# A recurrence's gates one weight chunk later, a compressor's tanh ahead of the second half of q and k, in a two-layer hybrid decoder

## Chip, cores and metric

One core of a Trainium2 chip. The time is device microseconds of one execution of the whole program; before the change the median of three runs is 248.72. The engines are named as the profile names them: PE (matrix products), DVE (vector engine), ACT (scalar engine), POOL and SP.

## The reference, cut to what matters

Two layers. Each makes one input projection and feeds two mixers from it: a gated recurrence of width 512 (RG-LRU) and an attention of 8 query heads and 2 key/value heads with three branches (compressed blocks, selected blocks, sliding window). Both are gated, joined and projected back onto the residual. SEQ is 256, D_MODEL 1024, everything float32.

```python
def rg_lru(x, w_r, b_r, w_i, b_i, lam):
    B, S, C = x.shape
    xb = x.reshape(B, S, RG_BLOCKS, RG_BLOCK)
    r = jax.nn.sigmoid(jnp.einsum('bsnc,ncd->bsnd', xb, w_r).reshape(B, S, C) + b_r)
    i = jax.nn.sigmoid(jnp.einsum('bsnc,ncd->bsnd', xb, w_i).reshape(B, S, C) + b_i)
    log_a = (-RG_C * r.astype(jnp.float32)) * jax.nn.softplus(-lam.astype(jnp.float32))
    a = jnp.exp(log_a)
    u = jnp.sqrt(-jnp.expm1(2.0 * log_a)) * (i * x).astype(jnp.float32)
    ...
    _, h = lax.associative_scan(combine, (a, u), axis=1)
    return h.astype(x.dtype)

def compress_blocks(blocks, pe, w1, w2):
    z = (blocks + pe).reshape(blocks.shape[:-2] + (CMP_LEN * HEAD_DIM,))
    return jax.nn.silu(z @ w1) @ w2

def hybrid_layer(x, norm_g, w_in, ...):
    h = rms_norm(x, norm_g)
    z = h @ w_in
    ...
    y_a = rg_lru(causal_depthwise_conv(rg_x, conv_w, conv_b), rg_wr, rg_br, rg_wi, rg_bi, rg_lam)
    y_a = y_a * jax.nn.silu(rg_gate)
    y_b = nsa(q, k_c, v_c, k_s, v_s, k_w, v_w, br_gate, q_g, k_g, ...)
    y_b = y_b * jax.nn.silu(nsa_gate)
    y = jnp.concatenate([y_a, y_b], axis=-1)
    return x + y @ w_out
```

With 256 positions there are 4 blocks of 64, and up to 16 may be chosen, so every block is selected, so the selected and the window branch attend to all earlier positions; the kernel computes both side by side.

## The kernel before

All of the weights stream through the core. A weight chunk is loaded by DMA, cut into a rounded high part and a low remainder (L170, a DVE operation of 128 x 1024 for most chunks), and multiplied in three passes (L175 to L177), which is what a `mm3` is: high by high, high by low, low by high.

A layer is a list of steps, one weight chunk each. First eight chunks `wt` give q and the keys token by token, then `wc` and `wv` the compressor's inputs and the values, then twelve chunks `wf` of 24 matmuls each, which give the recurrence's input (x0 to x3), the attention's gate (n0 to n3) and the recurrence's gate (g0 to g3), and at last eight chunks `wo` of the output projection. `SL` is the plan of the layer's small work: for each piece the number of the chunk, counted from the first `wf` chunk, in front of which it is given out (with `mid` after the loads, still ahead of the products). The lines 782 to 807 turn `SL` into lists, in the order in which `at` is called; two pieces with the same number stand in that order. The Tile layer then sorts the instructions of each engine by its own list scheduler, so the order in the program is not that of the source word for word, and each engine runs its list strictly in order.

The pieces that the change and the prediction's steps touch:

- `qk_transpose(t)`, for one half of the tokens: PE turns the keys (L371) and queries (L380); ACT rounds the keys twice (L375, L376) and the queries (L384, twice); DVE writes the low halves, `kl` (L377) and the lower 64 rows of `qs` (L385, twice); ACT copies the queries once more (`qT`, L387). In layer 0 the second half is given out in front of chunk 2, in layer 1 in front of chunk 1 (`SL["qk"][1] - l`).
- the compressor: `cmp_act` multiplies the hidden vectors by a selection matrix (L468, PE), takes a tanh (`hth`, L470, ACT) and the product `hs` (L472, DVE). `cmp_kv` multiplies `hs` by the second weights (L477, L478, PE) and normalises the compressed keys (L482 to L495); `cmp_kt` turns them (L499, L501). `cmp_scores` (L511 to L533) and `cmp_pt` (L538, and a copy `pct`, L83) follow. In `SL` these three are `cmp=(2, 3, 4)`.
- `att_scores`: scores of a head pair (L581 to L583 on PE, reading `kd`, `kl` and all of `qs`), the negated maximum (L586, L588, DVE), the exponential (L594, ACT). `att_coef`: L599 and L600 on DVE, then the scaling L609 on ACT. `att_turn`: transposes L622 and copies L83. `att_out`: L636 to L642 and L644.
- the recurrence: `rg_x(j)` frees the projection's PSUM bank (L654, DVE) and convolves (L655 ACT, three L657 DVE). `rg_gates(j)`: two products L665 on PE, four functions on ACT (L668, L669, L671, L672), and for odd j L675 and L678 on DVE and a square, L677, on ACT. `rg_sqrt`: one square root of 128 x 1024 on ACT (L681), for which a table is loaded (ACT_TABLE_LOAD) and another one loaded back before the next exponential. Then the scan (L686) and the gated output (L690).

PSUM banks: the chunk products and the gate products share the two banks `fm` in turn; `m` is one bank, `pp` two, `s` three.

Of the kernel before, what the change touches and what calls it, by code (L numbers as in the profile page):

```python
# [38 lines left out]
for _n, _w in (("g", 8), ("cw", 16), ("cb", 4), ("br", 4), ("bi", 4), ("lam", 4)):  # L39
# [12 lines left out]
K = dict(scale="A", ev1="A", hid="A", pct="A")  # L52
SL = dict(qk=(0, 2), order=("x0", "x1", "x2", "x3", "n0", "n1", "g0", "g1", "g2", "g3", "n2", "n3"),
          cmp=(2, 3, 4), att=(1, 3, 3, 4, 6, 7, 10, 11), turn=(3, 4, 5, 6, 8, 10,
          12, 13), cs=(5, 5), cpt=6, aout=(7, 15), gates=(2, 3, 4, 5), tab=6, sqrt=5,
          scan=8, rout=(9, 11))


# [13 lines left out]
def hybrid_trunk_kernel(ctx: ExitStack, tc: tile.TileContext, vx, wc, wt, wv, wf, wo, w1, w2, pe,  # L72
# [185 lines left out]
    def layer(l, prev):  # L258
# [520 lines left out]
        def at(n, f, *a, mid=False):  # L779
            plan[n][1 if mid else 0].append(F(f, *a))  # L780

        at(1, cmp_hid)
        at(SL["qk"][0], qk_transpose, 0)
        at(SL["qk"][1] - l, qk_transpose, 1)
        for n, f in zip(SL["cmp"], (cmp_act, cmp_kv, cmp_kt)):
            at(n, f)
        for q in range(8):
            i, t = divmod(q, 2)
            n = SL["att"][q]
# [34 lines left out]
    for l in range(DEPTH):  # L824
        prev, st_ = layer(l, prev)
        prev0 = prev0 or prev
        steps += st_
# [140 lines left out]
```

## Time and profile before

| | us |
|---|---|
| median of three runs | 248.72 (248.48 to 249.34) |
| the profiled execution, its own time | 248.43 |
| its span in the trace | 246.6 |
| PE busy in the span | 240.6 |
| DVE busy | 195.6 |
| ACT busy | 163.8 |

The span is what the trace covers from the first to the last instruction; 1.83 us of the profiled execution lie around it. Busy times overlap, since the engines work side by side. A share of PE near one says that a matmul was in its pipe nearly always, also while the next one was held back a little. The clock that PE was granted is at its full level in all forty slices of the page.

### The profile page before, as it was taken

What the parts mean: (1) busy time and instruction counts of PE and PEld (TensorE: products, weight loads), DVE (VectorE), ACT (ScalarE), POOL (GpSimd) and SP (SyncE); (2) the same over time, 40 slices, a digit from 0 to 9 for tenths busy, and PEclk for the clock granted to TensorE, in tenths of its full rate; (3) what the DMA queues carried; (4) which work ended last, traced back from release to release, by engine and by line L of the source; (5) the groups of instructions that cost most, each with busy time, mean ns of one, the idle gap of its engine ahead of it and who ended that gap; (6) DMA issues with size and microseconds to landing.
All of it is one profiled execution on the core that took longest, in us unless ns stands there. A gap on an engine that the chain in (4) does not pass through costs nothing.

```text
span 246.6 us, 5201 instructions
## 1 busy us (share of the span) xinstructions
PE 240.6 (98%) x1958; PEld 222.2 (90%) x1958; DVE 195.6 (79%) x379; ACT 163.8 (66%) x414; POOL 38.8 (16%) x65
## 2 busy tenths in 40 slices
PE   8999999989999999999999999999999999999994
PEld 3989998978998899979999999987899979998993
DVE  5997897999999988555995569699997999865322
ACT  6965529799999878523863453778999998760100
POOL 0035450012600011000001044101100101110000
PEclk9999999999999999999999999999999999999999
DMA  6988999774789388851479878558559675870022
GB/s 219 358 296 267 347 412 406 258 237 144 248 321 403 116 287 309 244 167 48 144 227 350 306 237 255 182 170 241 193 187 346 229 258 159 292 229 6 3 85 85
DMA packets 17593, 57.17 MB, mean 232 GB/s; under 512 B 2208, under 2 KB 3360, under 8 KB 17056
## 3 DMA queue, kind: packets, MB, share of 16 engines
q1 hardware_dynamic: 12816, 39.86, 46.8%
q0 software_dynamic: 4608, 16.78, 21.5%
q8 instruction: 15, 0.25, 0.4%
q10 hardware_dynamic: 144, 0.20, 0.2%
q14 instruction: 10, 0.08, 0.1%
HBM read 55.78 MB, written 1.05 MB: 230 GB/s over the span
## 4 chain that ended last, share of the span: by engine, by line
PE 81%; DVE 10%; ACT 4%; issue 2%; DMA 1%; DVEq 0%; ACTq 0%
PE fm L175 14%; PE fm L177 13%; PE fm L176 13%; PE pp L622 4%; PE s L176 4%; PE s L177 4%; PE s L175 4%; PE m L636 3%; DVE wl L170 2%; PE s L582 2%; PE s L581 2%; PE fm L665 2%; DVE qs L385 2%; PE pp L177 2%; PE pp L176 2%
## 5 line engine op out<-in xcount | busy, mean ns | idle before, releaser
L170 DVE TENSOR_TENSOR wl<-raw,wh 128x1024 fp32r<-128x1024 f32 (+4 forms) x67 | 74.3, 1114 | 7.8 <-PE pp L176 2.9
L175 PE MATMUL fm<-hh,wh 128*128 128x256 f32 x192 | 56.9, 296 | 0.1
L177 PE MATMUL fm<-hh,wl 128*128 128x256 f32 x192 | 54.7, 285 | 0.0
L176 PE MATMUL fm<-hl,wh 128*128 128x256 f32 x192 | 54.6, 285 | 0.0
L167 ACT CAST wh<-raw 128x768 fp32r<-128x768 f32 (+4 forms) x34 | 30.4, 898 | 26.3 <-DMA raw<-in_wc_dram 6.8
L175 PEld LDWEIGHTS fm<-hh,wh 128*128 128x128 f32 x192 | 36.7, 191 | 1.9 <-issue 1.2
L176 PEld LDWEIGHTS fm<-hl,wh 128*128 128x128 f32 x192 | 36.7, 191 | 0.2
L177 PEld LDWEIGHTS fm<-hh,wl 128*128 128x128 f32 x192 | 36.7, 191 | 0.2 <-DVE wl L170 0.2
L594 ACT ACTIVATE pr<-s,sm 128x128 f32<-128x128 f32 (+1 forms) x64 | 26.2, 424 | 2.7 <-DVE sm L588 1.9
L175 PE MATMUL fm<-yy,wh 128*128 128x256 f32 x96 | 27.4, 285 | 0.0
L176 PE MATMUL fm<-yy,wh 128*128 128x256 f32 x96 | 26.8, 279 | 0.0
L177 PE MATMUL fm<-yy,wl 128*128 128x256 f32 x96 | 26.8, 279 | 0.0
L609 ACT ACTIVATE pr<-pr,sm 128x128 f32<-128x128 f32 (+1 forms) x64 | 23.9, 458 | 2.3 <-DVE sm L600 2.3
L175 PEld LDWEIGHTS fm<-yy,wh 128*128 128x128 f32 x96 | 18.0, 188 | 0.8 <-issue 0.8
L156 POOL DMA_DIRECT2D wh<-in_wo_dram x16 | 8.4, 527 | 62.7 <-PE fm L177 28.0
L176 PEld LDWEIGHTS fm<-yy,wh 128*128 128x128 f32 x96 | 18.1, 188 | 0.0
L177 PEld LDWEIGHTS fm<-yy,wl 128*128 128x128 f32 x96 | 18.0, 188 | 0.0
L156 POOL DMA_DIRECT2D wh<-in_wf_dram x16 | 9.0, 563 | 49.7 <-PE fm L177 17.0
L176 PE MATMUL s<-wl,hh 128*128 128x384 f32 x48 | 16.5, 344 | 0.3 <-DVE wl L170 0.3
L177 PE MATMUL s<-wh,hl 128*128 128x384 f32 x48 | 16.2, 337 | 0.0
L175 PE MATMUL s<-wh,hh 128*128 128x384 f32 x48 | 15.5, 346 | 0.0
L731 DVE TENSOR_TENSOR head<-head,fm 128x512 f32<-128x512 f32 x11 | 7.5, 686 | 9.7 <-PE fm L177 9.6
(206 smaller groups left out, 612.6 us busy)
## 6 DMA issues: line engine op xcount, KB each, us to landing
raw<-in_wf_dram SPq DMA_DIRECT2D x24, 512.0 KB, 4.9
wh<-in_wf_dram POOLq DMA_DIRECT2D x16, 512.0 KB, 4.9
raw<-in_wo_dram SPq DMA_DIRECT2D x16, 512.0 KB, 5.3
wh<-in_wo_dram POOLq DMA_DIRECT2D x16, 512.0 KB, 5.0
raw<-in_wt_dram SPq DMA_DIRECT2D x15, 384.0 KB, 4.1
yy<-in_w_dram SPq DMA_DIRECT2D x4, 1024.0 KB, 7.0
raw<-in_wc_dram SPq DMA_DIRECT2D x4, 512.0 KB, 4.8
raw<-in_wv_dram SPq DMA_DIRECT2D x4, 420.0 KB, 4.6
```

The lines of the kernel that those rows point to most:

```text
L156: G.dma_start(self.wh, self.src)
L167: A.copy(hi[:, c], self.raw[:, c])
L170: V.tensor_tensor(lo[:, c], self.raw[:, c], hi[:, c].bitcast(F32), op=ALU.subtract)
L175: T.matmul(o, lh, rh, start=start, stop=False)
L176: T.matmul(o, lh, rl, start=False, stop=False)
L177: T.matmul(o, ll, rh, start=False, stop=stop)
L385: L.qk_done[t] = V.tensor_tensor(L.qs[HD:, g::2, tok], src, L.qs[:HD, g::2, tok].bitcast(F32), op=ALU.subtract)
L594: A.activation(pr[g][:, b], ov[:, b], AF.Exp, bias=sm[:, 0, 2 * g + b:2 * g + b + 1], accum_out=sm[:, 1, 2 * g + b:2 * g + b + 1])
L609: A.activation(pr[g][:, b], pr[g][:, b], AF.Copy, scale=sc_)
L622: T.transpose(pp[:, (2 * g + b) * P:(2 * g + b + 1) * P], pr[g][:, b, c * P:(c + 1) * P], ident)
L636: T.matmul(o[g * HD:(g + 1) * HD], L.vv[:, 0, b, g * HD:(g + 1) * HD], pt[:, g, b, 0:2].rearrange("p a s -> p (a s)"), start=h == b == 0, ...
L731: V.tensor_tensor(x_sb[:, m], x_sb[:, m], os_[0].rearrange("p (a s) -> p a s", a=2), op=ALU.add)
```

## The change

The `wf` chunks 2 to 5 (counted from 0) had one gate step each ahead of them (`gates=(2, 3, 4, 5)`); these four steps go one chunk further on, and the square root with them, from 5 to 6. Apart from that, `cmp_act` keeps its number but is given out before the second half of `qk_transpose` instead of behind it. In layer 1 the second half of q and k is already one chunk ahead of `cmp_act`, so there the second part of the diff changes nothing.

```diff
--- before.py
+++ after.py
@@ -52,7 +52,7 @@
 SL = dict(qk=(0, 2), order=("x0", "x1", "x2", "x3", "n0", "n1", "g0", "g1", "g2", "g3", "n2", "n3"),
           cmp=(2, 3, 4), att=(1, 3, 3, 4, 6, 7, 10, 11), turn=(3, 4, 5, 6, 8, 10,
-          12, 13), cs=(5, 5), cpt=6, aout=(7, 15), gates=(2, 3, 4, 5), tab=6, sqrt=5,
+          12, 13), cs=(5, 5), cpt=6, aout=(7, 15), gates=(3, 4, 5, 6), tab=6, sqrt=6,
           scan=8, rout=(9, 11))
@@ -781,8 +781,9 @@
         at(1, cmp_hid)
         at(SL["qk"][0], qk_transpose, 0)
+        at(SL["cmp"][0], cmp_act)
         at(SL["qk"][1] - l, qk_transpose, 1)
-        for n, f in zip(SL["cmp"], (cmp_act, cmp_kv, cmp_kt)):
+        for n, f in zip(SL["cmp"][1:], (cmp_kv, cmp_kt)):
             at(n, f)
```

What becomes of it in the engines' lists is seen at three places. On PE in layer 0, in front of the third `wf` chunk (+ is the changed kernel, - the kernel before; the line numbers up to L783 are the same in both):

```order
 L177 MATMUL fm<-hh,wl 128x256
+L468 MATMUL m<-cst,hid 128x160
 L371 MATMUL pp<-cst,pt 128x128 x2
 L380 MATMUL pp<-cst,pt 128x128 x4
-L468 MATMUL m<-cst,hid 128x160
-L665 MATMUL fm<-cx,rws 128x256 x2
```

The hidden vectors' product goes ahead of the six transposes, and the first gate's two products leave this place.

On DVE in layer 0, at the same time:

```order
 L654 TENSOR_TENSOR xpad_72<-fm,rb 128x256
 L600 TENSOR_TENSOR sm<-gate,sm 128x4
+L472 SCALAR_TENSOR_TENSOR hs<-hth,m 128x160
+L657 SCALAR_TENSOR_TENSOR cx<-xpad_72,head,cx 128x256
 L377 TENSOR_TENSOR kl<-pp,kd_122 64x2x128
 L657 SCALAR_TENSOR_TENSOR cx<-xpad_72,head,cx 128x256
```

`hs` is now ahead of the low halves of the keys and queries (L377, L385); before, it stood behind both L385.

On ACT in layer 0 around the square root, before the change:

```order
L594 ACTIVATE pr,sm<-s,sm 128x128
L681 ACT_TABLE_LOAD
L681 ACTIVATE tl<-tl 128x1024
L83 COPY pct<-m 128x256
L83 COPY pt<-pp 128x4x128 x2
L609 ACTIVATE pr<-pr,sm 128x128 x4
L594 ACT_TABLE_LOAD
L594 ACTIVATE pr,sm<-s,sm 128x256 x4
```

and after it:

```order
L83 COPY pt<-pp 128x4x128 x2
L668 ACTIVATE rr<-fm,hb 128x256
L669 ACTIVATE tmp_998<-fm,hb 128x256
L83 COPY pct<-m 128x256
L671 ACTIVATE tl<-rr,sp 128x256
L594 ACTIVATE pr,sm<-s,sm 128x256
L672 ACTIVATE rr<-rr,sp 128x256
L609 ACTIVATE pr<-pr,sm 128x128
L677 ACTIVATE tmp_1076<-rr 128x512
L609 ACTIVATE pr<-pr,sm 128x128 x3
L681 ACT_TABLE_LOAD
L681 ACTIVATE tl<-tl 128x1024
```

The table load and the square root stand behind the copies `pct` and `pt`, the fourth gate's functions and the scaling of a head pair, instead of in front of them.

## Rows read from the trace of the kernel before

**Rows 1.** The page: busy us of each engine, share of span, instructions.

```profile
PE 240.6 (98%) x1958; PEld 222.2 (90%) x1958; DVE 195.6 (79%) x379; ACT 163.8 (66%) x414; POOL 38.8 (16%) x65
```

**Rows 2.** Waits of PE: engine line, waited for: us in total, times, longest.

```profile
PE m L113 <- DVE wz L110: 1.1, 1, 1.1
PE m L477 <- DVE hs L472: 0.8, 1, 0.8
```

**Rows 3.** Timeline of PE, layer 0: start us, us, engine, line, what.

```profile
47.44 1.03 PE L665 MATMUL fm<-cx,rws 128*128 128x256 f32 x4
48.12 0.47 PE L175 MATMUL fm<-hh,wh 128*128 128x256 f32 x1
48.42 0.28 PE L176 MATMUL fm<-hl,wh 128*128 128x256 f32 x1
...
51.06 0.28 PE L177 MATMUL fm<-hh,wl 128*128 128x256 f32 x1
51.18 0.40 PE L581 MATMUL s<-kd,qs 128*128 128x512 f32 x1
52.42 0.30 PE L477 MATMUL m<-w2s,hs 128*32 128x64 f32 x2 [0.85 <-DVE hs L472]
...
53.26 0.48 PE L581 MATMUL s<-kd,qs 128*128 128x512 f32 x1
```

**Rows 4.** Timeline of ACT, same stretch.

```profile
49.95 0.30 ACT L470 ACTIVATE hth<-m 128x160 f32<-128x160 f32 x1
50.15 0.47 ACT L668 ACTIVATE rr<-fm,hb 128x256 f32<-128x256 f32 x1
50.64 0.58 ACT L384 CAST qs<-pp 64x512 fp32r<-64x512 f32 x1
```

**Rows 5.** Timeline of DVE, same stretch.

```profile
51.32 0.69 DVE L385 TENSOR_TENSOR qs<-pp,qs 64x512 fp32r<-64x512 f32 x1
52.05 0.32 DVE L472 SCALAR_TENSOR_TENSOR hs<-hth,m 128x160 f32<-128x160 f32 x1
```

**Rows 6.** Busy us by stretch: PE, PEld, DVE, ACT, POOL, PEclk, DMA share, GB/s.

```profile
60.00:70.00 10.00, 10.00 (x82) 9.04 (x81) 9.90 (x18) 10.00 (x32) 5.19 (x11) 1.00 0.75 241
...
100.00:110.00 10.00, 10.00 (x95) 9.21 (x96) 6.16 (x7) 3.28 (x6) 0.53 (x1) 1.00 0.68 202
```

**Rows 7.** Timeline of PE, the same place in layer 1.

```profile
165.98 1.03 PE L665 MATMUL fm<-cx,rws 128*128 128x256 f32 x4
167.09 0.39 PE L175 MATMUL fm<-hh,wh 128*128 128x256 f32 x1
...
170.16 0.30 PE L477 MATMUL m<-w2s,hs 128*32 128x64 f32 x2
...
170.63 0.48 PE L581 MATMUL s<-kd,qs 128*128 128x512 f32 x1
...
171.23 0.48 PE L581 MATMUL s<-kd,qs 128*128 128x512 f32 x1
```

**Rows 8.** Timeline of PE, layer 0: first output products, next pair's transposes.

```profile
78.60 0.65 PE L636 MATMUL m<-pt,vv 128*64 128x256 f32 x4
...
89.58 1.04 PE L622 MATMUL pp<-cst,pr 128*128 128x128 f32 x8
```

**Rows 9.** Timeline of DVE, layer 1.

```profile
166.61 0.42 DVE L654 TENSOR_TENSOR xpad<-fm,rb 128x256 f32<-128x256 f32 x1
...
169.75 0.31 DVE L472 SCALAR_TENSOR_TENSOR hs<-hth,m 128x160 f32<-128x160 f32 x1
```

**Rows 10.** Timeline of ACT, layer 0, round the square root.

```profile
75.47 0.20 ACT L594 ACTIVATION_READ_ACCUMULATOR pr<-s,sm 128x1 f32 x1
75.70 1.28 ACT L681 ACT_TABLE_LOAD   x1
76.99 1.06 ACT L681 ACTIVATE tl<-tl 128x1024 f32<-128x1024 f32 x1
77.96 0.35 ACT L83 COPY pct<-m 128x256 f32<-128x256 f32 x1
```

**Rows 11.** Timeline of ACT, layer 1, gate functions.

```profile
185.32 0.52 ACT L668 ACTIVATE rr<-fm,hb 128x256 f32<-128x256 f32 x1
...
186.53 0.55 ACT L609 ACTIVATE pr<-pr,sm 128x256 f32<-128x256 f32 x1
```

**Rows 12.** Timeline of ACT, layer 0, scaling of the next head pair.

```profile
86.47 1.71 ACT L609 ACTIVATE pr<-pr,sm 128x256 f32<-128x256 f32 x4 [1.26 <-DVE sm L600]
```

## The prediction, made before the changed kernel was run

> **What bounds the kernel now.** I read the busy shares first, then what the Tensor engine (PE) waited for, and then the timelines round those waits. The page gives PE 240.6 of the 246.6 us span [rows 1]. That share counts a matmul that is in the pipe, so it says only that PE is the engine to watch; what PE lost is found in its waits. Beside the warm-up at the start, one wait of PE on another engine is near a microsecond: L477, the compressor's second product, waits 0.8 us for `hs` of the Vector engine (DVE) [rows 2]. It lies in layer 0: the scores' first matmul starts at 51.18, L477 at 52.42, where matmuls otherwise follow each other by 0.12 [rows 3]. Nobody else delayed that much; so what the change can win lies here and in small delays.
>
> Why was `hs` late? On the Scalar engine (ACT) the tanh L470 ran at 49.95, behind the copies of the second half of q and k, and the recurrence's first tanh L668 (0.49 from start to start) then stood in front of the second L384 at 50.64 [rows 4]. DVE, which works its list in order, took L385 (waiting for that L384) at 51.32 and only then L472 (`hs`) at 52.05 [rows 5]. Both helpers are full: from 60 to 70 us DVE is busy 9.90 of 10 and ACT 10.00; from 100 to 110 they are at 6.16 and 3.28 [rows 6]. Work that PE doesn't need soon can therefore be put off, up to a point.
>
> **The change, part by part: layer 0.** Two things are taken from in front of `hs`: its matmul L468 now precedes the transposes L371 and L380, with the tanh ahead of the casts on ACT and `hs` ahead of both L385; and the first gate's product (0.68 us on PE, 47.44 to 48.12 [rows 3]) with its four functions goes one chunk later. `hs` then needs L470 and a 0.32 us DVE operation early in the chunk, some 2 us before PE wants it. That stall is gone. What is late next is the second half of the queries. PE can start the chunk at 47.44 and needs 3.06 for it (48.12 to 51.18 [rows 3]), so 50.50. The two compressor products take 0.47 and the first score group 0.60 (170.16 to 170.63 to 171.23, the same work in layer 1 [rows 7]); two transposes take about 0.2 (a quarter of what eight take, 1.04 with the end of the pipe [rows 8]). PE thus stands at the second score group at 51.77, and that reads what the second L385 writes. L385 ended at 52.01 before [rows 5]. In the new order `hs` (0.32) is ahead of it, which could make it 52.3; on ACT the tanh still precedes, but L668's 0.49 is gone, which could make it 51.7. I take 52.1, since DVE is the fuller chain: a new wait of about 0.3, between 0 and 0.55. Before, the same group began at 53.26 [rows 3], with the gate's 0.68 already done and the two transposes not: 53.26 - 0.68 + 0.2 = 52.78. Gain 52.78 - 52.1 = 0.7, between 0.5 and 1.0.
>
> Something is given back. The new order cuts PE's work into more pieces: the second gate's two products are parted by L499 and a score group, the first head's transposes stand in two pairs, the eight transposes of the next head in four pairs between scores, and L538 falls inside a run of weight matmuls; I count six new breaks. A return to weight matmuls costs at most 0.18 (48.12 to 48.42 is 0.30, against 0.12 from 51.06 to 51.18 [rows 3]), and may cost nothing where the other product is as long as its load: 0 to 1.1 in all. Most of these breaks lie between transposes and scores, not before weight matmuls, so I take 0.05 each, 0.3. Layer 0: 0.7 - 0.3 = 0.4 faster.
>
> **Layer 1.** There L468 already stood early, and only the gates move. Before, the first gate's product and the wait behind it took 1.11 (165.98 to 167.09 [rows 7]), 0.43 more than 0.68: the third x chunk's bank was being read by L654, which ended at 167.03 [rows 9]. In the new order that chunk uses the other bank and starts at 165.98. With 3.07 (167.09 to 170.16) and one score group of 0.60 that now stands ahead, PE is at L477 at 169.65. But `hs` ends at 170.06, held by DVE's own list [rows 9], which doesn't change up to there. So PE waits 0.41: the removed wait comes back under another name. By 170.1 PE has done 0.60 of scores in place of 0.68 of gate: no gain, no loss. Later the order has up to two breaks fewer; I take 0.05 faster, at most 0.36.
>
> **What costs nothing, and what hides it.** The fourth gate's functions and the square root now come after the first copies of the output stage. The copy of `pct` on ACT ended at 78.31 and PE read it at 78.60 [rows 8, 10]: 0.29 of cover. PE now comes there eleven matmuls, 1.3 us, sooner, but ACT no longer has the table load and square root (75.70 to 77.96, 2.26 us [rows 10]) ahead of that copy, and has two of the gate's functions instead (0.8 by [rows 11]: two of three that take 1.21). Net cover about 0.3 + 2.26 - 0.8 - 1.3 = 0.45; without it PE would pay what is missing. The scan's results are wanted only by the output projection, far behind. No DMA is moved to another queue, and the Pool engine's order is the same.
>
> The sum: 0.4 + 0.05 = 0.45 faster. Against the profiled execution's own 248.43 that is 247.98; its span is 246.6, with 1.83 around it that I leave as it is. That execution is 0.29 below the median of the runs, 248.72, to which I apply the same difference: 248.27, rounded to **248.3**. About 0.3%, 0.75 us, is what a measurement of this kernel can tell from no change, so the forecast is "the same".
>
> **The rivals.** *Nothing is given back.* The qs half comes by 51.77, the breaks are free and layer 1 saves its 0.36: 1.0 + 0.36 = 1.36 faster, 247.4; for this speaks that the order has work at hand at each break, against it the DVE at 9.9 of 10 [rows 6].
>
> *The square root pushes the next head pair's exponentials (slower).* The switch pair now stands behind the fourth gate. Three gate functions took 1.21 (185.32 to 186.53 [rows 11]); four and the pair's square, at 0.4 each, are 2.0. The exponentials behind the second table load, then the scaling L609 and at last the transposes L622 would come up to 2.0 later. L609 ended at 88.18 (86.47 + 1.71 [rows 12]) and PE began those transposes at 89.58 [rows 8]: 1.40 of cover. Beyond that PE waits, up to 0.6 in each layer, and if the 0.45 cover of `pct` goes with it since it hangs on the same ACT list, another 0.4: 1.6 in all, 1.6 - 0.45 = 1.15 slower, 249.9. For it speaks ACT's full list [rows 6]; against it that ACT had 1.26 us of idle just before that L609 [rows 12], which would take up most of it. It decides from a slip of 1.4 us.
>
> *The chip pays more for a switch at its new place.* A table load took 1.28 at 75.70, and the ACT instruction before it ended at 75.67 [rows 10], so nothing but the load is seen. Were each of the four switches to cost its 1.28 once more, past the cover, the time would be 248.3 + 5.1 = 253.4. The Trainium skill, ScalarE: Activation LUTs (What ACT_TABLE_LOAD costs), says that a switch pays a drain of about 1.38 us beside the load of 1.28; by that an estimate for four switches would be 5.5 us more. The trace agrees with its load, and shows no such drain.
>
> *It doesn't do what it says.* `hs` comes early, but L385 comes so much later that PE stands as long as before: 248.7.
>
> **How the numbers follow.** Forecast 0.55 (own range 247.8 to 249.3: a gain of 1.0 with breaks of 0.2 at the one end, of 0.5 with breaks of 1.1 at the other). Nothing given back 0.27; square root 0.12; switch 0.02; no effect 0.04. The range goes from 247.4, the first rival, to 249.6, short of the full price of the second, which leaves about 2 in 10 out. Faster by over 0.3%: 0.27 and 0.03 of the forecast's lower edge, 0.30. Slower: 0.12 + 0.02 + 0.03 of its upper edge, 0.17. Within: 0.53.
>
> **What would show it.** Right: no wait of L477 on `hs` in layer 0, and a short one of a score matmul L581 on L385 there; in layer 1 a wait of about 0.4 of L477 on `hs` and none of L175 on L654. Wrong: a PE wait on L609 behind the square root, or on the copy of `pct`; or, if faster, no wait at L581. If the time is over 249.6 with none of these, my count of breaks is wrong.

## The result, and the profile of the changed kernel

The changed kernel takes 250.55 us (median of five runs, 250.04 to 251.27) against 248.63 for the kernel before in the same measurement: a ratio of 1.0066, interval 1.0046 to 1.0087. It is slower by 1.9 us in the medians and 1.6 by the ratio, where 248.3 was forecast and the range ended at 249.6. Its profiled execution took 250.04, with a span of 248.2.

The page still shows PE as the engine that is nearly always busy (busy us of each engine, share, instructions), which says as little as it did before [rows 1]:

```profile
PE 242.1 (98%) x1958; PEld 222.5 (90%) x1958; DVE 194.4 (78%) x379; ACT 164.1 (66%) x414; POOL 39.4 (16%) x65
```

The waits of PE (us in total, times, longest) look harmless too; `L477` still waits for `hs`, though not where it did [rows 2]:

```profile
PE m L113 <- DVE wz L110: 1.1, 1, 1.1
PE m L477 <- DVE hs L472: 0.5, 1, 0.5
PE s L176 <- DVE wl L170: 0.2, 1, 0.2
PE s L581 <- DVE qs L385: 0.2, 1, 0.2
```

Beside the wait at the start, which was there before, no wait of a microsecond stands in this list, so the list is not enough. What finds it is to follow the same matmul through both traces. The weight matmuls stand in the same order in all programs here, so the first one of a chunk marks a stage. The first row gives the time of each mark in the trace of before, the other rows how much longer each stage took than there (us; "after again" is a second trace of the changed kernel, e1 to e10 are the experiments below).

| kernel | start to first `wf` | layer 0, to first `wo` | to third `wo` | to layer 1's first `wf` | layer 1, to first `wo` | to third `wo` | median of runs |
|---|---|---|---|---|---|---|---|
| before (time of the mark) | 37.05 | 97.75 | 104.31 | 155.52 | 215.67 | 222.23 | 248.6 |
| after | +0.23 | -0.29 | **+1.01** | 0.00 | +0.29 | +0.36 | 250.55 |
| after again | +1.03 | -0.25 | **+1.04** | +0.03 | +0.30 | +0.36 | 250.22 |
| e1 tanh only | +0.02 | +0.41 | 0.00 | 0.00 | -0.01 | 0.00 | 248.82 |
| e2 gates only | +0.59 | +0.48 | +1.11 | 0.00 | +0.29 | +0.35 | 250.65 |
| e3 gate 4, sqrt back | +0.09 | +1.35 | 0.00 | 0.00 | +1.33 | +0.37 | 251.53 |
| e4 sqrt only | +0.29 | +0.01 | +0.37 | 0.00 | +0.14 | 0.00 | 249.17 |
| e5 coefficients first | +0.16 | -0.28 | +0.23 | 0.00 | +0.30 | +0.47 | 249.40 |
| e7 layer 0 only | -0.10 | -0.02 | +0.23 | 0.00 | +0.01 | 0.00 | 248.56 |
| e8 short scan | -0.10 | -0.23 | +0.37 | 0.00 | +0.29 | 0.00 | 249.02 |
| e9 hs early in layer 1 | -0.06 | -0.29 | +0.23 | +0.10 | -0.01 | +0.32 | 248.82 |
| e10 the same, other end | +0.14 | -0.28 | +0.23 | 0.00 | -0.02 | +0.49 | 249.19 |

What follows the third `wo` chunk of layer 1 is within 0.02 of before in every trace. The first stage lies ahead of every instruction that the change moves, and its scatter (0.23 and 1.03 in two traces of one and the same program) is chance. The same goes for the first `wf` chunk of layer 0, the beginning of the second stage: in all these programs the order on every engine is that of before up to 46 us. The rest of the changed kernel adds up to -0.29 + 1.01 + 0.29 + 0.36 = 1.37, in its second trace to 1.48. So the gain in layer 0 is there, and more than it is lost in three places: at the end of that layer (1.01), in the middle of layer 1 (0.29) and at its end (0.36).

**The stretch that costs most.** PE in front of the second `wo` chunk of layer 0, before (timeline: start us, us, engine, line, what):

```profile
97.75 0.36 PE L175 MATMUL fm<-yy,wh 128*128 128x256 f32 x1
...
100.63 1.03 PE L622 MATMUL pp<-cst,pr 128*128 128x128 f32 x8
101.42 0.37 PE L175 MATMUL fm<-yy,wh 128*128 128x256 f32 x1
```

and after:

```profile
97.69 0.36 PE L175 MATMUL fm<-yy,wh 128*128 128x256 f32 x1
...
100.88 1.74 PE L622 MATMUL pp<-cst,pr 128*128 128x128 f32 x8
102.37 0.36 PE L175 MATMUL fm<-yy,wh 128*128 128x256 f32 x1
```

From 97.69 to 102.37 are 4.68 us, against 3.67 before. The eight transposes come 0.3 later behind the first matmul shown (3.19 in place of 2.88) and take 1.49 to the next matmul in place of 0.79. They read what the scaling L609 writes. On ACT, before:

```profile
97.11 0.21 ACT L594 ACTIVATION_READ_ACCUMULATOR pr<-s,sm 128x1 f32 x1
97.83 1.71 ACT L609 ACTIVATE pr<-pr,sm 128x256 f32<-128x256 f32 x4 [0.50 <-DVE sm L600]
```

and after:

```profile
98.25 0.47 ACT L594 ACTIVATE pr<-s,sm 128x256 f32<-128x256 f32 x1
98.61 0.20 ACT L594 ACTIVATION_READ_ACCUMULATOR pr<-s,sm 128x1 f32 x1
98.70 0.58 ACT L83 COPY pt<-pp 128x512 f32<-128x512 f32 x1
99.17 0.65 ACT L546 ACTIVATE sgn<-tmp 128x512 f32<-128x512 f32 x1
100.31 1.71 ACT L609 ACTIVATE pr<-pr,sm 128x256 f32<-128x256 f32 x4 [0.50 <-DVE sm L600]
```

Before, this L609 started at 97.83, so 2.8 us ahead of PE's first transpose; now it starts 0.57 ahead, and PE is paced by its four parts of some 0.4 us each. L609 waits for the coefficients L600 of the last head pair. DVE, after:

```profile
96.95 1.22 DVE L170 TENSOR_TENSOR wl<-raw,wh 128x1024 fp32r<-128x1024 f32 x1
98.09 0.68 DVE L544 TENSOR_TENSOR tmp<-fm,rb 128x512 f32<-128x512 f32 x1
98.84 0.18 DVE L599 RECIPROCAL sm<-sm 128x4 f32<-128x4 f32 x1
98.93 1.21 DVE L170 TENSOR_TENSOR wl<-raw,wh 128x1024 fp32r<-128x1024 f32 x1
100.06 0.16 DVE L600 TENSOR_TENSOR sm<-gate,sm 128x4 f32<-128x4 f32 x1
```

and before:

```profile
97.36 0.18 DVE L599 RECIPROCAL sm<-sm 128x4 f32<-128x4 f32 x1 [0.80 <-ACT pr L594]
97.57 0.16 DVE L600 TENSOR_TENSOR sm<-gate,sm 128x4 f32<-128x4 f32 x1
```

L600 is 2.5 us later. Some 1.5 of that go with the exponentials L594, whose sums L599 needs and which end 1.5 later (98.81 against 97.32). The other 1.0 come from one weight split, L170, that now stands between L599 and L600 in DVE's list (1.22 from L599 to L600 in place of 0.21), and which PE does not need yet.

What went ahead of that? The busy windows (us; PE, PEld, DVE, ACT, POOL busy, each with its instructions, then PE's clock, DMA share, GB/s), before:

```profile
77.00:83.00 6.00, 6.00 (x60) 4.76 (x60) 5.78 (x12) 5.97 (x14) 0.00 (x0) 1.00 0.63 237
83.00:100.00 17.00, 17.00 (x142) 16.36 (x141) 14.58 (x25) 13.32 (x42) 2.64 (x5) 1.00 0.79 263
```

After:

```profile
77.00:83.00 6.00, 6.00 (x62) 4.76 (x60) 2.61 (x6) 5.95 (x13) 0.05 (x1) 1.00 0.53 184
83.00:100.00 17.00, 17.00 (x142) 16.36 (x141) 16.93 (x28) 13.70 (x41) 2.59 (x5) 1.00 0.73 231
```

From 77 to 83 us DVE, which worked 5.78 us before, works 2.61: it waits for the fourth gate's square on ACT, for the output products, and for the square root (waits of DVE there):

```profile
DVE tl L678 <- ACT tmp L677: 1.5, 1, 1.5
DVE cx L682 <- ACT tl L681: 0.9, 1, 0.9
DVE tmp L644 <- PE m L642: 0.9, 1, 0.9
```

The product with the root (L682, at 82.60 in place of 78.46) and the four scans behind it then fall into the next 17 us, where DVE has 16.93 us of work and no gap left to catch up in. The change took work from a full stretch of DVE, left a hole, and put the work into a stretch that had just 2.4 us to spare. The trace shows this backlog; it doesn't show whether the backlog made the coefficients late, or the order that the scheduler gave to the work.

### The profile page after: what moved, and what is told of

Same layout as the page of the kernel before. It is cut to its first block, busy times and chain, and to the rows that moved or that the text cites. A ratio compares the mean times of both kernels' runs of the same rounds, so it can differ in the third digit from the quotient of the medians.

```text
span 248.2 us, 5193 instructions
## 1 busy us (share of the span) xinstructions
PE 242.1 (98%) x1958; PEld 222.5 (90%) x1958; DVE 194.4 (78%) x379; ACT 164.1 (66%) x414; POOL 39.4 (16%) x65
## 4 chain that ended last, share of the span: by engine, by line
PE 65%; DVE 16%; ACT 13%; issue 2%; DMA 2%; SPq 0%; DVEq 0%; ACTq 0%
PE fm L175 10%; PE fm L176 10%; PE fm L177 10%; DVE wl L170 5%; PE s L176 4%; PE s L177 4%; PE s L175 4%; PE pp L622 3%; PE fm L665 2%; PE m L636 2%; ACT pr L609 2%; ACT pr L594 2%; DVE qs L385 2%; DMA raw<-in_wt_dram 2%; PE s L581 2%
## 5 line engine op out<-in xcount | busy, mean ns | idle before, releaser
L170 DVE TENSOR_TENSOR wl<-raw,wh 128x1024 fp32r<-128x1024 f32 (+4 forms) x67 | 74.2, 1112 | 7.0 <-PE pp L176 3.8
L175 PE MATMUL fm<-hh,wh 128*128 128x256 f32 x192 | 57.0, 297 | 0.0
L175 PEld LDWEIGHTS fm<-hh,wh 128*128 128x128 f32 x192 | 36.7, 191 | 1.4 <-issue 1.2
L594 ACT ACTIVATE pr<-s,sm 128x128 f32<-128x128 f32 (+1 forms) x64 | 26.1, 423 | 2.2 <-DVE sm L588 1.9
L175 PE MATMUL fm<-yy,wh 128*128 128x256 f32 x96 | 27.3, 285 | 0.0
L609 ACT ACTIVATE pr<-pr,sm 128x128 f32<-128x128 f32 (+1 forms) x64 | 24.2, 460 | 3.0 <-DVE sm L600 3.0
L175 PEld LDWEIGHTS fm<-yy,wh 128*128 128x128 f32 x96 | 18.1, 188 | 0.8 <-issue 0.8
L562 ACT CAST yy<-tmp 128x512 fp32r<-128x512 f32 x8 | 5.0, 622 | 17.8 <-DVE tmp L644 12.7
```

The source lines that it names most:

```text
L170: V.tensor_tensor(lo[:, c], self.raw[:, c], hi[:, c].bitcast(F32), op=ALU.subtract)
L175: T.matmul(o, lh, rh, start=start, stop=False)
L562: A.copy(L.yy[:, 0, k], yt)
L594: A.activation(pr[g][:, b], ov[:, b], AF.Exp, bias=sm[:, 0, 2 * g + b:2 * g + b + 1], accum_out=sm[:, 1, 2 * g + b:2 * g + b + 1])
L609: A.activation(pr[g][:, b], pr[g][:, b], AF.Copy, scale=sc_)
```

## The experiments

**First theory (A): the later square root and scan.** B held that the compressor's move cuts PE's work into more pieces, C that the first three gates' delay costs. Four kernels undo or do one part; each diff below says against which kernel it is.

*e1, the compressor's tanh and product alone (against the changed kernel):*

```diff
-          cmp=(2, 3, 4), ..., gates=(3, 4, 5, 6), tab=6, sqrt=6,
+          cmp=(2, 3, 4), ..., gates=(2, 3, 4, 5), tab=6, sqrt=5,
```

> Only the compressor's tanh and product go ahead of the second half of q and k; gates and square root stay at (2, 3, 4, 5) and 5. Theory A: the loss comes from the later square root and scan, which put the coefficients of the last head pair (L599, L600 on DVE) late, so that the scaling L609 on ACT and the transposes L622 on PE wait, 1.0 us in layer 0 and 0.4 in layer 1. By A this kernel has none of that wait, keeps the gain on hs in layer 0, and takes 248.0 to 248.5 (before: 248.63). Theory B: the loss comes from the reordering that the compressor's move brings, PE's work being cut into more pieces. By B it takes 249.5 or more. Theory C: the first three gates, one chunk later, are what costs (in layer 1 the wait of L477 on hs). By C it takes 248.0 to 248.6 too.

Measured: 248.82, ratio 1.0007 (0.9997 to 1.0016), no difference. B falls, there is no loss from this move. But there is no gain either, so that the time lies above the range of A and C, though `hs` comes early and L477 waits for nothing in layer 0 (PE):

```profile
51.66 0.30 PE L477 MATMUL m<-w2s,hs 128*32 128x64 f32 x2
...
53.51 0.50 PE L581 MATMUL s<-kd,qs 128*128 128x512 f32 x1 [0.53 <-DVE qs L385]
```

The second score group waits instead, for the second half of the queries. It was held on DVE by ACT's L384:

```profile
52.76 0.69 DVE L385 TENSOR_TENSOR qs<-pp,qs 64x512 fp32r<-64x512 f32 x1 [0.83 <-ACT qs L384]
```

In the changed kernel the same L385 starts at 51.79 (below). Taken alone, the move does what the prediction's last rival said: the stall changes its name. In these traces the two parts of the change are worth something in layer 0 only together. (The +0.41 of e1 and +0.48 of e2 in the table arose in the first `wf` chunk, 0.38 and 0.54; behind it they stand at +0.03 and -0.07, the changed kernel at -0.30.)

*e2, gates and square root alone (against the kernel before):*

```diff
-          ... gates=(2, 3, 4, 5), tab=6, sqrt=5,
+          ... gates=(3, 4, 5, 6), tab=6, sqrt=6,
```

> Only the gates (3, 4, 5, 6) and the square root (6) move; the compressor's tanh stays behind the second half of q and k. Theory A: 250.3 to 251.2, with L622 in front of the output projection waiting for L609 by about 1.0 us in layer 0 and 0.4 in layer 1, and besides L477 still waiting for hs in layer 0. Theory B: 248.2 to 248.8. Theory C: 250.3 to 251.2 as well.

Measured: 250.65, ratio 1.0088 (1.0073 to 1.0103), and +1.11 and +0.35 at the two ends of layers. The whole loss is in the gates and the square root.

*e3, the fourth gate and the square root put back (against the changed kernel):*

```diff
-          ... gates=(3, 4, 5, 6), tab=6, sqrt=6,
+          ... gates=(3, 4, 5, 5), tab=6, sqrt=5,
```

> The changed kernel with the fourth gate and the square root put back: gates (3, 4, 5, 5), square root 5. The order on DVE from the square root to the residual of layer 0 is then that of before. Theory A: no wait of L622 on L609 in front of the output projection; what stays is the gain on hs in layer 0 and the wait of L477 on hs in layer 1 (0.66): 248.2 to 248.8. Theory B: 249.8 to 250.6. Theory C: 249.3 to 250.6, since the first three gates stay late.

Measured: 251.53, ratio 1.0121 (1.0106 to 1.0135), which no theory expected. The loss at the end of layer 0 is gone, as A says (0.00), that of layer 1 is not (0.37), and two gates in one chunk brought a wait of their own (PE):

```profile
PE fm L175 <- ACT tmp L669: 2.1, 2, 1.3
```

Each takes a `fm` bank, and the next chunk's products wait until ACT has read it. The kernel shows this price of two gates in a row; for A against C it decides little.

*e4, the square root alone (against the kernel before):*

```diff
-          ... gates=(2, 3, 4, 5), tab=6, sqrt=5,
+          ... gates=(2, 3, 4, 5), tab=6, sqrt=6,
```

> The kernel before with the square root alone one chunk later (6); gates and compressor as before. Theory A: slower, 249.5 to 250.5, with L622 waiting for L609 in front of the output projection in both layers, since the coefficients L599 and L600 of the last head pair now stand on DVE behind a weight split L170 and the gate's L547. Theories B and C: 248.4 to 248.9, no such wait.

Measured: 249.17, ratio 1.0027 (1.0017 to 1.0038), outside every range. The direction is A's, the size a third of it: +0.37 at the end of layer 0, none at that of layer 1. In layer 0 L599 and L600 stand behind L544 and L170 here too (DVE):

```profile
97.89 0.69 DVE L544 TENSOR_TENSOR tmp<-fm,rb 128x512 f32<-128x512 f32 x1 [0.90 <-PE fm L177]
98.50 1.21 DVE L170 TENSOR_TENSOR wl<-raw,wh 128x1024 fp32r<-128x1024 f32 x1
99.64 0.17 DVE L599 RECIPROCAL sm<-sm 128x4 f32<-128x4 f32 x1
...
100.30 0.15 DVE L600 TENSOR_TENSOR sm<-gate,sm 128x4 f32<-128x4 f32 x1
```

The first `wo` matmul starts at 98.05, so the coefficients end 2.40 behind it, nearly as late as in the changed kernel (2.53; in the kernel before 0.02 ahead of it). Yet DVE had time: it waited 0.90 for PE ahead of L544, and was busy 15.12 of the 17 us from 83 to 100. So the later root alone brings the late coefficients in layer 0, through the order that the scheduler then makes. That they cost less here goes with PE's own order, in which the transposes are spread between weight matmuls:

```profile
101.11 0.44 PE L622 MATMUL pp<-cst,pr 128*128 128x128 f32 x2
101.30 0.36 PE L175 MATMUL fm<-yy,wh 128*128 128x256 f32 x1
101.51 0.44 PE L622 MATMUL pp<-cst,pr 128*128 128x128 f32 x2
```

**Second theory (A2): a full DVE queue, and the coefficients' place in it.** Rival D: ACT is late by itself, through table loads, root and exponentials, and DVE only follows.

*e5, the changed kernel with the last head pair's coefficients ahead of L544 and one weight split:*

```diff
+            L.coef = V.tensor_tensor(sm[:, 3]..., L.gate[:, t, i, :, 1:3], ...)
...
+                with tc.issue_after(L.coef.ins) if i == 3 else nullcontext():
+                    silu_gate(L.sgn[:, i - 1:i + 1])
...
+                if half == 1 and n == 0:
+                    c.after = lambda: L.coef
```

> The changed kernel with one order on DVE altered at the end of each layer's wf chunks: the coefficients of the last head pair (L600, L601 here) go ahead of the gate product L544 and of one weight split L170, which in the changed kernel stand between them. Theory A2: the later square root leaves DVE waiting at 77 to 82.6 us and then with 18 us of work without a gap, and the loss comes where the last head pair's coefficients stand in that queue behind work that PE does not need yet. By A2 they are done by about 99.0 instead of 100.2, L609 can start by 99.2, and the wait of L622 in front of the output projection falls from 1.0 to under 0.2 in layer 0 and from 0.35 to under 0.1 in layer 1: 249.2 to 249.5 (the changed kernel: 250.55). Theory D: ACT itself is late (table loads, square root and exponentials pushed back), DVE only follows. By D the wait stays within 0.3 of what it was: 250.2 to 250.7.

Measured: 249.40, ratio 1.0030 (1.0019 to 1.0040): 0.8 us less than the changed kernel in the same measurement (e6, 250.22), by a change of order alone. DVE now has:

```profile
98.77 0.18 DVE L600 RECIPROCAL sm<-sm 128x4 f32<-128x4 f32 x1 [0.68 <-ACT pr L595]
98.98 0.16 DVE L601 TENSOR_TENSOR sm<-gate,sm 128x4 f32<-128x4 f32 x1
```

(lines are one further on here) and ACT's scaling starts at 99.24. In layer 0 the loss falls from 1.01 to 0.23, while the exponentials end as late as in the changed kernel and PE's transposes stand eight in a row as there. So 0.78 of the 1.01 is the place of the coefficients in DVE's list, and D, which left the wait within 0.3 of what it was, falls for that part. In layer 1 A2 missed: 0.47 in place of under 0.1. There the scaling came early enough, but PE then waited for the copies L83 of the transposed scores, which stand behind it and behind L546 on ACT.

*e6, the changed kernel once more, with nothing edited:*

> The changed kernel once more, nothing edited, for a second trace of it. The stages behind the first wf chunk should repeat within 0.1: -0.3 in layer 0 up to the output projection, +1.0 in front of it, +0.3 and +0.35 in layer 1. If the start of the program (up to the second wf chunk, 43.5 us in the trace of before) is what varies between executions, it differs here from the +0.24 of the first trace; median 250.2 to 250.9.

Measured: 250.22 (249.79 to 250.91), ratio 1.0059 (1.0042 to 1.0076). All stages behind the start repeat within 0.04; the start takes 0.8 longer than in the first trace.

*e7, the change in layer 0 alone, with the coefficients first there:*

```diff
-            at(SL["gates"][i], rg_gates, i)
+            at(SL["gates"][i] - l, rg_gates, i)
...
-        at(SL["sqrt"], rg_sqrt, mid=True)
+        at(SL["sqrt"] - l, rg_sqrt, mid=True)
```

(and e5's edit for l == 0)

> The change in layer 0 alone (layer 1 keeps gates (2, 3, 4, 5) and square root 5), with the coefficients of the last head pair of layer 0 ahead of L544 and of one weight split. Theory A2: layer 1 is that of before (0.0), layer 0 keeps its 0.3 ahead of the output projection and loses at most 0.2 there: 248.3 to 248.7 against 248.66 before. Theory D: 249.3 to 249.8, with L622 still waiting about 1.0.

Measured: 248.56, ratio 0.9997 (0.9985 to 1.0010): as fast as before. Layer 1 costs 0.01, the end of layer 0 again 0.23, against D's 1.0.

*e8, the scan cut to 8 of 256 positions:*

```diff
-                V.tensor_tensor_scan(L.tl[:, j], L.rr[:, j], L.cx[:, j], 0.0, ALU.mult, ALU.add)
+                V.tensor_tensor_scan(L.tl[:, j, :8], L.rr[:, j, :8], L.cx[:, j, :8], 0.0, ALU.mult, ALU.add)
```

> The changed kernel with the scan L686 over the first 8 of 256 positions instead of all (the rest of the scan is left out), which takes some 2 us of DVE's work from behind the square root in each layer. Theory A2 (a full DVE queue is what makes the coefficients late): the wait of L622 in front of the output projection falls below 0.3 in layer 0 and below 0.1 in layer 1, 249.2 to 249.7, as the whole queue moves up. Theory D (ACT late by itself): no change there, 250.2 to 250.7.

Measured: 249.02, ratio 1.0016 (1.0006 to 1.0026), faster than A2's range. The loss is 0.37 in layer 0, above the 0.3 expected, and 0.00 in layer 1. This doesn't show that the queue's load is the cause, since with a shorter scan the scheduler made other orders. In layer 0 the coefficients come hardly sooner than in the changed kernel (DVE):

```profile
99.66 0.15 DVE L600 TENSOR_TENSOR sm<-gate,sm 128x4 f32<-128x4 f32 x1
```

With the first `wo` matmul at 97.41 that is again 2.40 behind it. At the ends of layers the loss goes with the order. The table gives times in us behind the layer's first `wo` matmul; where it names the same order, the instructions on PE, DVE and ACT stand in the same order from 4 us ahead of that matmul to 4 us behind it.

| order | where | scan | exponentials end | coefficients end | transposes on PE | loss |
|---|---|---|---|---|---|---|
| before's | before, both layers; e3, layer 0; e4, layer 1 | whole | -0.4 | 0.0 | eight in a row | 0.00 |
| before's | e8, layer 1 | cut | -0.4 | 0.0 | eight in a row | 0.00 |
| e4's | e4, layer 0; e3, layer 1 | whole | 0.8 | 2.4 | between weight matmuls | 0.37 |
| e4's | e8, layer 0 | cut | 0.8 | 2.4 | between weight matmuls | 0.37 |
| the changed kernel's | after, layer 0 | whole | 1.1 | 2.5 | eight in a row | 1.01 |

With the same order the whole scan and the cut one cost the same. What A2 says of the coefficients' place is shown by e5; what it says of the full queue is not.

**Layer 1's middle.** The changed kernel loses 0.29 there. e9 and e10 take away the wait of L477 on `hs`.

*e9:* e5, with

```diff
-        at(SL["cmp"][0], cmp_act)
+        at(SL["cmp"][0] - l, cmp_act)
```

> As e5_coef_first (the changed kernel with the last head pair's coefficients ahead), and in layer 1 the compressor's tanh and product given out one chunk earlier, in front of the second half of q and k, as the change does in layer 0. If the wait of L477 on hs in layer 1 (0.66 us in the changed kernel) is a plain loss on PE's path, it goes and the stage from the first to the tenth wf chunk of layer 1 falls from +0.28 to between -0.4 and -0.2 against before: 248.7 to 249.0 (e5: 249.40). If other work then waits in its place, as in e1 where the tanh alone gained nothing, the stage stays at 0.0 to +0.3 and the time at 249.1 to 249.5.

Measured: 248.82, ratio 1.0007 (0.9995 to 1.0019). The stage goes from +0.30 to -0.01, and L477 starts at 168.95 without a wait. The time fell in the range of a plain loss, but the stage lies between the two expectations: about half of the gain came. The rest of the time comes from the end of layer 1, which cost 0.32 and not 0.47.

*e10:* e9, with e5's edit in layer 0 alone.

> As e9_hs_layer1, but in layer 1 the coefficients of the last head pair keep the place that the scheduler gives them (in e5 the edit there moved the wait of L622 from L609 to the copies L83 and made it 0.47 in place of 0.35). With the layer 0 of e5, the middle of layer 1 at -0.4 to -0.2 and its end at about +0.35: 248.6 to 248.9; if other work waits in place of hs, 249.0 to 249.4.

Measured: 249.19, ratio 1.0018 (1.0007 to 1.0029). The middle is that of e9 (-0.02), but the end of layer 1 costs 0.49, so the time is that expected for other work in place of `hs`. The coefficients end 2.52 behind the first `wo` matmul there, though no edit touched their place in layer 1 (1.87 in the changed kernel). That miss says that what the scheduler makes of the end of a layer can't be read off the place of one step. No version beat the kernel before by more than can be measured; e7 equals it.

## Why the prediction was wrong, by its steps

**Layer 0 up to the output projection: right.** Forecast 0.4 faster; measured 0.29 and 0.25. No wait of L477 on `hs` is left, and the new wait stands where it was expected, on L385 (PE, after; compare [rows 3]):

```profile
51.90 0.47 PE L622 MATMUL pp<-cst,pr 128*128 128x128 f32 x2
52.53 0.50 PE L581 MATMUL s<-kd,qs 128*128 128x512 f32 x1 [0.16 <-DVE qs L385]
```

```profile
51.79 0.69 DVE L385 TENSOR_TENSOR qs<-pp,qs 64x512 fp32r<-64x512 f32 x1
```

L385 ends at 52.48; less the 0.23 that this execution started late, 52.25, where 52.1 was taken [rows 5]. So the group's start gained 52.78 - 52.30 = 0.48 in place of 0.7, and the breaks took back about 0.2 in place of 0.3; both sizes were too large, which brought the difference close to the forecast. The traces of e1 and e2 add that neither part brings this alone, which the prediction, whose sum takes both from in front of `hs`, had not said.

**Layer 1: the mechanism right, the term mis-sized.** L175 no longer waits for L654, and L477 waits for `hs` instead, as forecast (after; compare [rows 7, 9]):

```profile
169.82 0.40 PE L581 MATMUL s<-kd,qs 128*128 128x512 f32 x1
...
171.09 0.30 PE L477 MATMUL m<-w2s,hs 128*32 128x64 f32 x2 [0.52 <-DVE hs L472]
```

```profile
170.72 0.32 DVE L472 SCALAR_TENSOR_TENSOR hs<-hth,m 128x160 f32<-128x160 f32 x1
```

The wait was sized 0.41; PE loses 0.69 (171.09, where 0.12 behind the last score matmul's start at 170.28 would have done). Part of that is only that PE comes sooner. The stage came out 0.29 slower where 0.05 faster stood. At the transposes behind these scores (172.63 before, 172.97 after, which is 0.61 earlier on the layer's own clock, with the gate's 0.68 still to do) the exchange is even, as predicted; the other 0.2 come later, where "up to two breaks fewer" was wrong. Which breaks these are was not tested. e9 shows that taking the wait on `hs` away is worth 0.31.

**What costs nothing: this step failed.** For the square root and scan it said that their results are wanted only by the output projection, far behind, and the sum put them at nothing. That looks at who reads the scan. It leaves out what the move does to the order of the other work on the engines: the coefficients of the last head pair, two short operations that PE needs at 100.6, ended 2.5 us later on DVE, and PE lost 1.01 in layer 0 and 0.36 in layer 1. The root alone brings the late coefficients in layer 0 (e4), and e5 gives 0.78 of the 1.01 back by putting them ahead of L544 and a weight split. The other 0.23 goes with the exponentials, which end 1.5 later; there the backlog on DVE may count, since the scan and 0.8 us of L682 moved behind 83 us, but no run separates it from the order. Rows that gave warning were at hand in the trace of before: DVE had some 2.4 us to spare from 83 to 100, and the L609 of the last pair stood 2.8 us ahead of PE. The busy windows chosen [rows 6] end at 70 and begin again at 100, on either side of the stretch that mattered. The copy of `pct`, to which the step gave its attention, was on time (done at 77.07, read at 77.22).

Of the signs of being wrong, the wait of PE on L609 behind the root came, though as a pacing inside the transposes that the list of waits of this trace doesn't name. The count of breaks, which the prediction would blame for a time over 249.6 without such a wait, can account for no more than the 0.2 in layer 1.

**The rival came true in kind, at another place.** "The square root pushes the next head pair's exponentials" named the chain that ended late, exponentials, L609, L622, with 249.9. It was priced at the transposes at 89.58 [rows 8, 12], where the slip turned out small: after, that L609 ends at 88.63 (86.92 + 1.71) and PE comes at 89.53, so 0.9 of cover are left. The loss came one pair later, 11 us on, through the coefficients on DVE. So 0.12 was too low a chance, and the range should not have stopped at 249.6, short of this rival's own price.

**The switch: refuted.** ACT round the square root, after (compare [rows 10]):

```profile
79.47 0.72 ACT L609 ACTIVATE pr<-pr,sm 128x128 f32<-128x128 f32 x2
80.21 1.28 ACT L681 ACT_TABLE_LOAD   x1
81.50 1.06 ACT L681 ACTIVATE tl<-tl 128x1024 f32<-128x1024 f32 x1
82.58 1.28 ACT L594 ACT_TABLE_LOAD   x1
```

The load takes 1.28 as before and starts 0.02 after the work ahead of it; nothing else is paid at the new place. The Trainium skill, ScalarE: Activation LUTs (What ACT_TABLE_LOAD costs), speaks of a drain beside the load; this trace shows the load and no drain.

**What stays open.** The stages behind the start add up to 1.4 and 1.5 us. The medians differ by 1.9 and 1.7, but the ratios, 1.6 (1.1 to 2.2) and 1.5 us (1.0 to 1.9), have these sums in their intervals. Not shown are how much of the 1.5 us by which the exponentials are late is DVE's backlog, which breaks cost layer 1 its other 0.2, and why e4 is 0.14 slower in the middle of layer 1.

## What to carry to other kernels

When a step is put off, don't ask only who reads its result; look at the order that the scheduler makes of everything behind it, and above all at short operations that the busiest engine is waiting for: behind which long ones do they stand, and how far ahead of their deadline? Here one place in DVE's list was worth 0.78 us. Before a difference between two kernels is put down to the operation that was edited, compare the orders on all engines: the shorter scan and the later root each brought a new order on PE as well. To find a loss that no list of waits shows, mark stages by the same matmul in both traces and take differences; here a loss of 1 us appeared as transposes that were spread out, not as one wait.

## What the runs showed of the hardware that was not expected

One and the same operation on POOL takes one of two times. The reciprocal roots of the head norms, L181, 128 x 12, take 2.26 us each in seven of the twelve traces, but in five of them one of the four takes 3.25, in the changed kernel's second trace and not in its first (durations: least, median, longest in ns). After:

```profile
L181 POOL TENSOR_TENSOR st<-st,mhalf x4: 2262/2266/2292, 28.0 to 148.8; 128x12 f32<-128x12 f32 x4
```

After again:

```profile
L181 POOL TENSOR_TENSOR st<-st,mhalf x4: 2257/2280/3252, 28.5 to 149.7; 128x12 f32<-128x12 f32 x4
```

The reader agrees: in the second trace DVE waits 2.16 us for it (L347), in the first 1.14. In those five executions (e2, e3, e6, e7, e8), and in no other, PE then waits 0.5 to 0.8 us for a weight split L170 at the first `wf` chunk, since the split stands behind the normalisation on DVE. In the changed kernel's second trace, e7 and e8 that delay is made up for by shorter waits in the rest of layer 0's middle or nearly so; it blurs that column of the table by some tenths.
